# Two edits to an encoder layer: early residual rows stored through SP's queue, and the closing norm divided over VectorE, ScalarE and GpSimd

## The chip, the cores and the metric

The kernel runs on one core of one Trainium2 chip. A core has TensorE (PE, matmuls, with its weight loads shown apart as PEld), VectorE (DVE), ScalarE (ACT), GpSimd (POOL) and SyncE (SP). SP does no arithmetic here: it issues most of the DMAs, one after the other, in the order in which the program has them. GpSimd issues the indirect DMAs (gathers and scatters by a list of row numbers) and a few plain ones. The metric is device microseconds of one execution. The kernel before was timed three times: 889.92 us in the median (888.94 to 892.41).

## What is computed

One encoder layer on 1024 tokens of 1024 features, in float32:

```python
h  = x
hn = rms_norm(h, norm_mix_g);  proj = hn @ w_in            # q, k, v of both attentions
y_dil = dilated_mixture_attention(...)                      # 8 heads, 512 columns
y_na  = neighbourhood_attention(...)                        # 8 heads, 512 columns
h = h + concat(rms_norm(y_dil, g_out_dil), rms_norm(y_na, g_out_na)) @ w_out
h = h + hierarchical_moe(rms_norm(h, norm_ffn_g), ...)      # each token: 2 of 16 SwiGLU experts
return rms_norm(h, norm_final_g)                            # row * 1/sqrt(mean(row^2) + eps) * g
```

## The kernel before

A matmul is made of three: each operand is split into a high part (ScalarE, `L103`) and a low part (VectorE, or GpSimd for some weights, `L104`), and high x high, low x high and high x low are summed in PSUM. Tokens are handled in eight blocks of 128 rows; `acc_d` in DRAM holds the residual rows `h`.

**The output projection has two halves.** `early_out` (`L742` to `L762`) is the first: while the last attention heads run, it multiplies block T of `y_dil` with the upper half of `w_out`, 24 matmuls a block (`L750`), and VectorE adds the product to the x rows of the block (`L753`, two instructions of 512 columns). When a block is done, its rows go to `acc_d` by a plain DMA that GpSimd issues (`L760`), and then SP loads the x rows of block T + 2 (`x_load`, `L726`). The second half begins when the first has ended. Its function `load(T)` has SP read a block of `y_na` (two DMAs, `L1160`) and of `acc_d` (`L1163`); PE turns the `y_na` block by four transposes (`y_turn`, `L135`), ScalarE and VectorE split it, and 24 matmuls a block follow (`L1270`). Three blocks are loaded ahead, the next ones inside the loop.

**The order of the work is written out by hand.** The whole program is one straight order of statements, with no scheduler: an engine's instructions stand in its queue as the statements issue them, and each engine works off its queue in order. An instruction waits until the semaphores of what it depends on have come.

**The experts** run 16 in a row with PE as the busiest engine. Their rows are added to `acc_d` by indirect DMAs; the last two experts (14 and 15) add theirs in SBUF.

**The end of the kernel** is the final norm. Row blocks 0 to 7 are loaded from `acc_d`; blocks 8 to 11 are gathered rows of the tokens of experts 14 and 15 (two blocks each), to which the experts' last products are still added (`add_both`, `add_late`, `L1631`). For each block ScalarE sums the squares (`square`, `L1570`); an inverse root of their mean is formed, either on VectorE by a bit trick and three Newton steps (`inverse_root_steps`, for blocks 0 to 3) or as ScalarE's Sqrt and VectorE's reciprocal (the others); and `finish(t)` scales the rows by the root and by g in one VectorE instruction (`L1609`) and stores them. Blocks 0 to 5 are stored through SP (`L1613`). Blocks 6 and 7 go out by an indirect DMA of GpSimd that leaves out the tokens of experts 14 and 15 (the index `keep`), and blocks 8 to 11 by indirect DMAs as well (`put`, `L1461`), once the blocks stored through SP have landed.

Between them the statements of the last experts stand, so that their splits, adds and matmuls share the queues with the norm. A `bank` of PSUM with tag "o" exists twice: the two halves of one expert's product fill both, and the next product can't be begun before VectorE has added the earlier one (`L1631`).

Of the kernel before, what the change touches and what calls it, by code (L numbers as in the profile page):

```python
# [13 lines left out]
AF = mybir.ActivationFunctionType  # L14
ALU = mybir.AluOpType
# [57 lines left out]
def build(nc, tc, a, ctx, dbg=None):  # L73
# [21 lines left out]
    acc_d = dram("acc_d", [1024, 1024])  # L95
# [7 lines left out]
        nc.scalar.activation(hi, src, AF.Copy)  # L103
        (nc.gpsimd if pool else nc.vector).tensor_tensor(lo, src, f(hi), op=ALU.subtract)  # L104

    def inverse_root_steps(ss, r, t, scale):


        V = nc.vector
        V.tensor_scalar(ss, ss, scale, EPS, op0=ALU.mult, op1=ALU.add)  # L110
        yield
        V.tensor_scalar(r.bitcast(I32), ss.bitcast(I32), -0.5, float(0x5f3759df), op0=ALU.mult, op1=ALU.add)
        yield
        for _ in range(3):
            V.tensor_tensor(t, r, r, op=ALU.mult)
            yield
            V.scalar_tensor_tensor(t, t, -0.5, ss, op0=ALU.mult, op1=ALU.mult)
            yield
            V.scalar_tensor_tensor(r, t, 1.5, r, op0=ALU.add, op1=ALU.mult)
            yield  # L120

    def run(gen, n=1):
        for _ in range(n):
            next(gen, None)
# [20 lines left out]
    with ExitStack() as att:  # L145
# [27 lines left out]
        with ExitStack() as ph:  # L173
# [4 lines left out]
            def x_load(T):  # L178
                xs[T] = xp.tile([128, 1024], F32, name="xt", bufs=3)
                nc.sync.dma_start(xs[T], a["x"][0, T * 128:(T + 1) * 128, :])  # L180
# [519 lines left out]
        who, wlo, raws, yd, yt, hx = {}, {}, {}, {}, {}, {}  # L700
# [35 lines left out]
        def yd_rstd():  # L736

            yield from inverse_root_steps(rd, rr, rt_, 1.0 / 512)

        def early_out():  # L740

            for T in range(8):  # L742
                y = yt.pop(T)
                for c in range(2):
                    ps = bank("mm")
                    cc = slice(512 * c, 512 * c + 512)
                    i = 0
                    for k in range(4):
                        for l, w in ((0, who), (0, wlo), (1, who)):
                            nc.tensor.matmul(ps, y[:, l, k, :], w[0][:, k, cc], start=i == 0, stop=i == 11)  # L750
                            i += 1
                            if i == 12:
                                nc.vector.scalar_tensor_tensor(hx[T][:, cc], ps, rr[:, T:T + 1], hx[T][:, cc],  # L753
                                                               op0=ALU.mult, op1=ALU.add)
                            if T < 7 and 12 * c + i == 10:
                                yd_turn(T + 1)
                                if T < 5:
                                    yd_load(T + 3)
                            yield
                nc.gpsimd.dma_start(acc_d[128 * T:128 * T + 128, :], hx.pop(T))  # L760
                if T < 6:
                    x_load(T + 2)  # L762

        def g_out_load():
            for k, nm in ((0, "g_out_dil"), (4, "g_out_na")):
# [87 lines left out]
        for s in range(len(steps) + 4):  # L853
            at = s % 16
            before = pairs[s // 16 - 1] if s >= 16 else None
            if s < len(steps):
                p, h, n = steps[s]
# [83 lines left out]
    V = nc.vector  # L941
# [207 lines left out]
    with ExitStack() as ph:  # L1149
        op_ = ph.enter_context(tc.tile_pool(name="out", bufs=2))  # L1150
        y, h, yt, ht, rs, ry, pls = {}, {}, {}, {}, {}, {}, {}
# [212 lines left out]
    g_l = ex.tile([128, 1024], F32, name="g_l", bufs=1)  # L1364
# [60 lines left out]
    def act_in(act):  # L1425
        pt = bank("s")
        for k in range(2):
            nc.tensor.transpose(pt[:, k * 128:(k + 1) * 128], act[:, k * 128:(k + 1) * 128], ident)  # L1428
        ah = ex.tile([128, 256], F32R, name="a_hi")
        al = ex.tile([128, 256], F32R, name="a_lo")  # L1430
        split(ah, al, pt[:, 0:256])
        return ah, al
# [20 lines left out]
    def new_act():  # L1453
        return ex.tile([128, 256], F32, name="act", bufs=2)
# [30 lines left out]
    ss = ex.tile([128, 14], F32, name="ss_f", bufs=1)  # L1485
    hs, hr = {}, {}
# [82 lines left out]
    def square(t):  # L1569
        nc.scalar.activation(junk, hs[t // 2][:, t % 2], AF.Square, accum_out=ss[:, t:t + 1])  # L1570

    def inverse_root(*ts):
        c, n = ts[0], len(ts)
        r = ex.tile([128, 8], F32, name="r_f", bufs=2)[:, 0:n]
        tmp = ex.tile([128, 8], F32, name="t_f", bufs=1)[:, 0:n]
        for t in ts:
            hr[t] = r[:, t - c:t - c + 1]
        yield from inverse_root_steps(ss[:, c:c + n], r, tmp, 1.0 / 1024)

    def mean(*ts):  # L1580
        v = ss[:, ts[0]:ts[0] + len(ts)]
        V.tensor_scalar(v, v, 1.0 / 1024, EPS, op0=ALU.mult, op1=ALU.add)

    def inverse_root_last(*ts):
        c, n = ts[0], len(ts)
        v = ss[:, c:c + n]
        nc.scalar.activation(v, v, AF.Sqrt)
        r = ex.tile([128, 8], F32, name="r_l", bufs=3)
        V.reciprocal(r[:, 0:n], v)
        for t in ts:  # L1590
            hr[t] = r[:, t - c:t - c + 1]

    def late(t):

        return gi[:, t % 2, at(14 + (t - 8) // 2)]
# [3 lines left out]
    def put(idx, src, of_block):  # L1599
# [4 lines left out]
            tc.declare_no_dep(ins, before, reason="rows of other tokens")  # L1604
        indirect.append((ins, of_block))

    def finish(t, whole=False):
        h = hs[t // 2][:, t % 2]
        V.scalar_tensor_tensor(h, h, hr[t], g_l, op0=ALU.mult, op1=ALU.mult)  # L1609
        if t > 7:  # L1610
            put(late(t), h, False)
        elif whole or t < 6:
            stored.append(nc.sync.dma_start(a["out"][128 * t:128 * t + 128, :], h).ins)  # L1613
        else:
            put(keep[:, t:t + 1], h, True)
# [7 lines left out]
    def inverse_root_half():  # L1623
        nc.scalar.activation(ss[:, 13:14], ss[:, 13:14], AF.Sqrt, scale=1.0 / 1024, bias=ss[:, 12:13])
        r = ex.tile([128, 8], F32, name="r_l", bufs=3)
        V.reciprocal(r[:, 0:1], ss[:, 13:14])
        hr[11] = r[:, 0:1]
# [5 lines left out]
    def add_both(t, parts):  # L1633
        for z in range(2):
            add_late(t, z, parts[z])
# [40 lines left out]
    add_both(8, parts)  # L1676
    for t in range(4):
        square(t)
    acts[0] = new_act()
    expert_up(xs.pop(15), W[15], ws[:, 0, at(15)], acts[0])  # L1680
    run(inverse_root(0, 1, 2, 3), 100)
    square(8)
    square(4)
    finish(0)
    parts = [expert_down(aa, W[14], z) for z in range(2)]
    aa = act_in(acts[0])
    finish(1)
    add_both(9, parts)
    for t in (5, 6, 7, 9):
        square(t)  # L1690
    finish(2)
    acts[1] = new_act()
    expert_up(xs1, W[15], ws[:, 1, at(15)], acts[1])
    nc.scalar.activation(root, root, AF.Sqrt)
    mean(4, 5, 6, 7, 8, 9)
    inverse_root_last(4, 5, 6, 7, 8, 9)
    finish(3)
    parts = [expert_down(aa, W[15], z) for z in range(2)]
    aa = act_in(acts[1])
    add_both(10, parts)  # L1700
    square(10)
    finish(4)
    finish(5)
    parts = [expert_down(aa, W[15], z, tag="mm") for z in range(2)]
    mean(10)
    inverse_root_last(10)
    add_late(11, 0, parts[0])
    square_half(0)
    finish(8)
    add_late(11, 1, parts[1])  # L1710
    square_half(1)
    finish(6)
    finish(9)
    inverse_root_half()
    finish(11)
    finish(10)
    finish(7)

    ordered.close()

# [74 lines left out]
```

## Time and profile before

| | |
|---|---|
| three timed runs | 888.94, 889.92, 892.41 us |
| the profiled execution, its own time | 892.44 us |
| its span, from the first to the last instruction | 890.7 us |
| PE busy | 832.3 us (93% of the span) |
| PE weight loads | 693.2 us (78%) |
| DVE, ACT, POOL busy | 558.5 (63%), 510.0 (57%), 220.9 us (25%) |
| matmuls | 4492 |
| bytes moved by DMA | 168.72 MB |

The profiled execution is 2.5 us longer than the median of the timed ones. A matmul's end is modelled, so PE counts as busy while it streams; what one costs is read from the distance of the starts. The column PEclk gives the clock that TensorE was granted, as a share of 2.4 GHz: 1.00 is 2.4 GHz, 0.50 is 1.2 GHz. Line numbers are those of the kernel before; in the changed kernel the same statements stand up to 30 lines lower.

### The profile page before, as it was taken

Reading aid. Unit: us, or ns where it says so; the run is one execution under the profiler, and the core shown is the slowest. Engines: PE = TensorE matmul, PEld = TensorE weight load, DVE = VectorE, ACT = ScalarE, POOL = GpSimd, SP = SyncE. Lnnn points to the kernel's source line nnn. Section 1 sums busy time; section 2 is a strip of 40 time slices with the busy share of each in tenths; the row PEclk is TensorE's granted clock in tenths of the full one; section 3 lists DMA queues with packets and bytes.
Section 4 is the critical chain, followed back from the end, with each engine's and each line's share of the span. In section 5 each row is a group of like instructions: output and inputs, shape, how many; then the busy total and the mean of one; then the engine's idle time right before and its main releaser. Section 6 shows DMA issues by size and latency. Waiting matters only on the chain. (4 is left out here: it accounts for less than half of the span.)

```text
span 890.7 us, 13312 instructions
## 1 busy us (share of the span) xinstructions
PE 832.3 (93%) x4492; PEld 693.2 (78%) x4492; DVE 558.5 (63%) x1249; ACT 510.0 (57%) x1079; POOL 220.9 (25%) x180
## 2 busy tenths in 40 slices
PE   8999999989999999999898999999799999999880
PEld 5888878979889888878787887887577787777760
DVE  4551125776767767666677753677786566959573
ACT  5441127757667576677575633543585566858570
POOL 4001122221232302332411100000442344635403
PEclk8999999999999999999999999998999999999995
DMA  6855452314343141534346747995798987999663
GB/s 238 286 210 165 126 159 65 105 48 108 96 136 105 54 137 48 148 100 120 76 160 195 265 144 239 357 343 216 233 354 250 317 220 209 357 324 304 181 257 121
DMA packets 129919, 168.72 MB, mean 189 GB/s; under 512 B 14875, under 2 KB 101403, under 8 KB 129824
## 3 DMA queue, kind: packets, MB, share of 16 engines
q1 hardware_dynamic: 119904, 143.58, 49.8%
q0 software_dynamic: 9936, 24.16, 9.8%
q8 instruction: 41, 0.67, 0.3%
q14 instruction: 38, 0.31, 0.1%
HBM read 129.93 MB, written 47.47 MB: 199 GB/s over the span
## 5 line engine op out<-in xcount | busy, mean ns | idle before, releaser
L103 ACT ACTIVATE pt_hi<-ps_pt 128x512 fp32r<-128x512 f32 (+2 forms) x128 | 67.6, 528 | 70.8 <-PE ps_pt L509 41.7
L378 PE MATMUL ps_mm<-xhi,w_lo 128*128 128x512 f32 x256 | 105.1, 411 | 1.1 <-POOL w_lo L104 1.1
L378 PE MATMUL ps_mm<-xlo,w_hi 128*128 128x512 f32 x256 | 105.0, 410 | 0.0
L378 PE MATMUL ps_mm<-xhi,w_hi 128*128 128x512 f32 x256 | 102.9, 402 | 0.0
L104 DVE TENSOR_TENSOR pt_lo<-ps_pt,pt_hi 128x512 fp32r<-128x512 f32 (+2 forms) x128 | 77.2, 603 | 31.8 <-ACT pt_hi L103 31.1
L104 POOL TENSOR_TENSOR w_lo<-w_raw,w_hi 128x1024 fp32r<-128x1024 f32 x16 | 38.3, 2392 | 229.5 <-ACT w_hi L103 229.5
L424 DVE CUSTOM_DVE_ANT_0 p<-ps_s,bias 128x256 f32<-128x256 f32 (+1 forms) x192 | 81.8, 450 | 18.2 <-PE ps_s L411 10.8
L104 DVE TENSOR_TENSOR g_lo<-raw_up,g_hi 128x1024 fp32r<-128x1024 f32 x64 | 75.5, 1220 | 25.2 <-ACT g_hi L103 25.1
L1419 PE MATMUL ps_mm<-g_hi,x_hi 128*128 128x512 f32 x184 | 76.0, 413 | 0.5 <-ACT x_hi L103 0.5
L1419 PE MATMUL ps_mm<-g_hi,x_lo 128*128 128x512 f32 x184 | 74.2, 403 | 2.2 <-DVE x_lo L104 2.2
L1419 PE MATMUL ps_mm<-g_lo,x_hi 128*128 128x512 f32 x184 | 73.9, 402 | 0.0
L430 ACT ACTIVATE p<-p,stats 128x256 f32<-128x256 f32 x128 | 63.7, 500 | 9.6 <-DVE stats L424 9.1
L103 ACT ACTIVATE g_hi<-raw_up 128x1024 fp32r<-128x1024 f32 x64 | 64.4, 1067 | 1.8 <-DMA raw_up<-in_w_up 0.8
L411 PE MATMUL ps_s<-k_hh,q_s 128*128 128x256 f32 (+1 forms) x192 | 60.7, 324 | 4.0 <-DMA k_hh<-k_hh 1.4
L411 PE MATMUL ps_s<-k_low,q_s 128*128 128x256 f32 (+1 forms) x192 | 62.6, 334 | 0.0
L411 PEld LDWEIGHTS ps_s<-k_hh,q_s 128*128 128x128 f32 x192 | 44.6, 232 | 10.9 <-DVE q_s L402 2.6
L378 PEld LDWEIGHTS ps_mm<-xhi,w_lo 128*128 128x128 f32 x256 | 48.7, 190 | 5.2 <-POOL w_lo L104 1.4
L1357 POOL DMA_INDIRECT xg<-hn_d,gi x30 | 41.3, 1377 | 40.1 <-PEq L1533 9.3
L378 PEld LDWEIGHTS ps_mm<-xhi,w_hi 128*128 128x128 f32 x256 | 48.7, 190 | 3.2
L378 PEld LDWEIGHTS ps_mm<-xlo,w_hi 128*128 128x128 f32 x256 | 48.4, 189 | 3.5
L411 PEld LDWEIGHTS ps_s<-k_low,q_s 128*128 128x128 f32 x192 | 44.6, 232 | 3.5
L430 ACT ACTIVATE p<-p,nm 128x384 f32<-128x384 f32 (+1 forms) x64 | 37.5, 586 | 15.2 <-DVE nm L424 14.8
(301 smaller groups left out, 2125.6 us busy)
## 6 DMA issues: line engine op xcount, KB each, us to landing
raw_up<-in_w_gate SPq DMA_DIRECT2D x32, 512.0 KB
raw_up<-in_w_up SPq DMA_DIRECT2D x32, 512.0 KB
raw_down<-in_w_down SPq DMA_DIRECT2D x16, 1024.0 KB
w_raw<-in_w_in SPq DMA_DIRECT2D x16, 512.0 KB
xt<-in_x SPq DMA_DIRECT2D x8, 512.0 KB
k_hh<-in_w_in SPq DMA_DIRECT2D x8, 512.0 KB
va_d<-vt SPq DMA_DIRECT2D x16, 256.0 KB
vb_d<-vt SPq DMA_DIRECT2D x8, 512.0 KB
```

The lines of the kernel that those rows point to most:

```text
L103: nc.scalar.activation(hi, src, AF.Copy)
L104: (nc.gpsimd if pool else nc.vector).tensor_tensor(lo, src, f(hi), op=ALU.subtract)
L378: nc.tensor.matmul(ps, l[:, k, :], x[half][:, k, :], start=i == 0, stop=i == 23)
L411: nc.tensor.matmul(ps, self.q[h][:, qs], keys(k[h]), start=n == 0, stop=n == 1)
L424: nc.vector.tensor_tensor_reduce(out=p, in0=ps, in1=bias, scale=-0.125, scalar=3.0e38, op0=ALU.add, op1=ALU.min, accum_out=nm)
L430: nc.scalar.activation(p, p, AF.Exp, bias=nm, scale=-1.0, accum_out=l)
L1357: return nc.gpsimd.indirect_dma_start(out=x, out_offset=None, in_=src[:, :], in_offset=bass.IndirectOffsetOnAxis(ap=idx, axis=0), bounds_c ...
L1419: nc.tensor.matmul(ps, l[:, k, :], wt[:, k, :], start=i == 0, stop=i == 23)
```

## The change

1. **Rows stored through SP.** `early_out` no longer issues the store of block T from GpSimd at the end of the block. A new function `h_store(T)` issues it, and the x load after it, from SP, at the seventh matmul of block T + 1; block 7's store is issued when the loop has ended.
2. **Newton steps on GpSimd.** For blocks 0 to 3 the three Newton steps (nine VectorE instructions) become twelve GpSimd instructions of 128x4; the first two instructions of the root stay on VectorE.
3. **g ahead of the root.** For blocks 0, 1, 4, 5 and 8 VectorE multiplies the rows by g as soon as the squares are summed (`times_g`), and `finish` is then one ScalarE instruction that scales by the root. The other blocks finish as before.
4. **Order and destinations.** Blocks 2 to 7 are stored through SP, and blocks 0 and 1 go out with the index `keep`. The order of the statements changes: finish 2, 3, 4, 6, 5, 7, 0, 9, 8, 11, 1, 10 in place of 0, 1, 2, 3, 4, 5, 8, 6, 9, 11, 10, 7.

```diff
-    def inverse_root_steps(ss, r, t, scale):
+    def inverse_root_steps(ss, r, t, scale, pool=False):
...
         for _ in range(3):
+            if pool:
+                for o, a, b in ((t, r, r), (t, t, ss), (t, None, None), (r, r, t)):
+                    if a is None:
+                        nc.gpsimd.tensor_scalar(t, t, -0.5, 1.5, op0=ALU.mult, op1=ALU.add)
+                    else:
+                        nc.gpsimd.tensor_tensor(o, a, b, op=ALU.mult)
+                    yield
+                continue
             V.tensor_tensor(t, r, r, op=ALU.mult)
...
+        def h_store(T):
+            nc.sync.dma_start(acc_d[128 * T:128 * T + 128, :], hx.pop(T))
+            if T < 6:
+                x_load(T + 2)
...
+                            if T and 12 * c + i == 6:
+                                h_store(T - 1)
...
-                nc.gpsimd.dma_start(acc_d[128 * T:128 * T + 128, :], hx.pop(T))
-                if T < 6:
-                    x_load(T + 2)
+            h_store(7)
...
+    def times_g(t):
+        h = hs[t // 2][:, t % 2]
+        V.tensor_tensor(h, h, g_l, op=ALU.mult)
+        by_g.add(t)
...
-        V.scalar_tensor_tensor(h, h, hr[t], g_l, op0=ALU.mult, op1=ALU.mult)
+        if t in by_g and not whole:
+            nc.scalar.activation(h, h, AF.Copy, scale=hr[t])
+        else:
+            V.scalar_tensor_tensor(h, h, hr[t], g_l, op0=ALU.mult, op1=ALU.mult)
...
-        elif whole or t < 6:
+        elif whole or t > 1:
...
-    run(inverse_root(0, 1, 2, 3), 100)
+    run(inverse_root(0, 1, 2, 3, pool=True), 100)
     square(8)
     square(4)
-    finish(0)
+    times_g(8)
     parts = [expert_down(aa, W[14], z) for z in range(2)]
     aa = act_in(acts[0])
-    finish(1)
+    times_g(4)
+    finish(2)
+    square(5)
     add_both(9, parts)
-    for t in (5, 6, 7, 9):
+    for t in (6, 7, 9):
         square(t)
-    finish(2)
+    finish(3)
...
```

SP's queue where the first half of the output projection ends, in the kernel before. `k_hh<-in_x` is an x load, `y_na<-y` a store of attention rows, and `y<-y_na` and `h<-acc_d` are the loads of the second half:

```order
L695 DMA y_na<-y 128x4x128 [waits DVE_49]
L695 DMA y_na<-y 128x4x128 [waits DMAHW0_49,DVE_49]
L726 DMA k_hh<-in_x 128x1024 [waits PE_49]
L1160 DMA y<-y_na 64x1x512 [waits DMAHW2_49,DMAHW3_49,DMAHW0_49,DMAHW5_49,PE_49,DMAHW7_49,Activation_49,Pool_49]
L1160 DMA y<-y_na 64x1x512
L1163 DMA h<-acc_d 128x1024 [waits DMAHW4_49]
```

The same place in the changed kernel, with the stores of blocks 5, 6 and 7 (`acc_d<-k_hh`):

```order
L703 DMA y_na<-y 128x4x128 [waits DVE_49] x2
L749 DMA acc_d<-k_hh 128x1024 [waits DMAHW6_49,DMAHW0_49]
L734 DMA k_hh<-in_x 128x1024 [waits PE_49]
L749 DMA acc_d<-k_hh 128x1024 [waits DMAHW3_49,DVE_49]
L749 DMA acc_d<-k_hh 128x1024 [waits DMAHW7_49,DMAHW1_49,DVE_49]
L1173 DMA y<-y_na 64x1x512 [waits DMAHW2_49,DMAHW4_49,PE_49,DMAHW5_49,Activation_49,Pool_49]
L1173 DMA y<-y_na 64x1x512
L1176 DMA h<-acc_d 128x1024
```

The stores of blocks 6 and 7 now stand ahead of the first `y_na` load, and each waits for VectorE.

GpSimd's queue at the end, in the changed kernel, from the last gather of rows on. In the kernel before the first `spacer` memset of `put` follows the gather directly:

```order
L1370 DMA raw_up<-acc_d,gi 128x1024
L120 TENSOR_TENSOR t_f<-r_f 128x4 [waits DVE_49]
L120 TENSOR_TENSOR t_f<-t_f,ss_f 128x4 [waits Activation_49,Pool_49]
L118 ISA
L118 TENSOR_SCALAR t_f<-t_f 128x4 [waits Pool_49]
L120 TENSOR_TENSOR r_f<-r_f,t_f 128x4 [waits Pool_49]
L120 TENSOR_TENSOR t_f<-r_f 128x4 [waits Pool_49]
L120 TENSOR_TENSOR t_f<-t_f,ss_f 128x4 [waits Pool_49]
L118 TENSOR_SCALAR t_f<-t_f 128x4 [waits Pool_49]
```

Besides the arithmetic there is one instruction more, `L118 ISA`, which the diff does not show. It is put in ahead of the first `tensor_scalar` of GpSimd and reloads the engine's library of instructions. The kernel before has one such instruction, `L104 ISA`, ahead of its first GpSimd `tensor_tensor` at the start.

VectorE's queue at the end, in the kernel before, right behind the last Newton step (`raw_down` and `raw_up` are row blocks, `g_l` is g, `a_lo` a split of the last experts):

```order
L1609 SCALAR_TENSOR_TENSOR raw_down<-raw_down,r_f,g_l 128x1024 [waits DMAHW7_49,DVE_49]
L104 TENSOR_TENSOR a_lo<-ps_s,a_hi 128x256 [waits Activation_49]
L1609 SCALAR_TENSOR_TENSOR raw_down<-raw_down,r_f,g_l 128x1024 [waits DMAHW0_49]
L1631 TENSOR_TENSOR raw_up<-ps_o,raw_up 128x512 [waits DMASW5_49]
L1631 TENSOR_TENSOR raw_up<-ps_o,raw_up 128x512
```

And in the changed kernel, from the last instruction of the root that stays on VectorE:

```order
L112 TENSOR_SCALAR r_f<-ss_f 128x4 [waits DVE_49]
L1622 TENSOR_TENSOR raw_up<-raw_up,g_l 128x1024 [waits Activation_49]
L104 TENSOR_TENSOR a_lo<-ps_s,a_hi 128x256 [waits Activation_49]
L1622 TENSOR_TENSOR raw_up<-raw_up,g_l 128x1024 [waits DMAHW3_49]
L1633 SCALAR_TENSOR_TENSOR raw_up<-raw_up,r_f,g_l 128x1024 [waits DMAHW1_49,Pool_49]
L1655 TENSOR_TENSOR raw_up<-ps_o,raw_up 128x512 [waits DMASW5_49]
L1655 TENSOR_TENSOR raw_up<-ps_o,raw_up 128x512
```

The finish of block 2 (`L1633`) waits for GpSimd, and the two adds that free the PSUM banks stand right behind it.

## Rows read from the trace of the kernel before

**Rows 1.** Busy time by stretch (engine busy and instructions, PEclk, DMA share, GB/s).
```profile
570.00:600.00 30.00, 30.00 (x187) 25.84 (x187) 21.88 (x67) 14.03 (x31) 0.00 (x0) 1.00 0.99 349
700.00:800.00 100.00, 98.60 (x464) 78.13 (x463) 63.40 (x79) 61.80 (x96) 46.10 (x32) 1.00 0.91 283
```

**Rows 2.** SP's timeline where the second half begins (start, length, issue, count).
```profile
534.44 1.36 SPq L1160 DMA_DIRECT2D y<-y_na  x2
...
540.89 0.46 SPq L1163 DMA_DIRECT2D h<-acc_d  x1
...
550.84 0.33 SPq L1243 DMA_DIRECT2D small<-in_small  x1
```

**Rows 3.** All engines' timeline at the same place; brackets: idle before, and its releaser.
```profile
540.68 0.60 PE L135 MATMUL ps_pt<-ident,y 128*128 128x128 f32 x4
...
540.88 0.75 DVE L753 SCALAR_TENSOR_TENSOR k_hh<-ps_mm,rr,k_hh 128x512 f32<-128x512 f32 x1 [2.05 <-PE ps_mm L750]
...
541.93 0.53 POOL L760 DMA_DIRECT2D acc_d<-k_hh  x1 [5.07 <-DVE k_hh L753]
...
542.37 0.51 PE L1270 MATMUL ps_mm<-whi,yt_hi 128*128 128x512 f32 x1 [1.09 <-ACT yt_hi L103]
```

**Rows 4.** Busy time just behind the first load's issue.
```profile
535.00:536.00 1.00, 1.00 (x6) 0.79 (x5) 0.72 (x1) 0.00 (x0) 0.00 (x0) 1.00 0.14 23
536.00:537.00 1.00, 1.00 (x6) 0.80 (x5) 0.04 (x1) 0.00 (x0) 0.53 (x1) 1.00 0.42 135
```

**Rows 5.** Busy time where PE stood still and began again.
```profile
832.00:833.00 1.00, 0.00 (x0) 0.00 (x0) 1.00 (x2) 1.00 (x4) 1.00 (x1) 1.00 0.78 66
...
834.00:836.00 2.00, 1.77 (x6) 1.48 (x7) 1.71 (x4) 1.22 (x2) 1.51 (x4) 0.62 0.91 141
...
838.00:840.00 2.00, 2.00 (x10) 1.62 (x9) 2.00 (x3) 0.95 (x1) 0.36 (x2) 1.00 0.82 285
```

**Rows 6.** The chain that ended last, same place (start, length, what).
```profile
834.74 7.08 PE ps_mm L1419 x24
...
845.71 5.61 PE ps_mm L1419 x24
```

**Rows 7.** VectorE's timeline in the closing norm.
```profile
852.38 0.17 DVE L112 TENSOR_SCALAR r_f<-ss_f 128x4 int32<-128x4 int32 x1
...
854.36 1.28 DVE L1609 SCALAR_TENSOR_TENSOR raw_down<-raw_down,r_f,g_l 128x1024 f32<-128x1024 f32 x1
...
857.09 1.28 DVE L1631 TENSOR_TENSOR raw_up<-ps_o,raw_up 128x512 f32<-128x512 f32 x2
...
870.63 0.68 DVE L1631 TENSOR_TENSOR raw_up<-ps_mm,raw_up 128x512 f32<-128x512 f32 x1
```

**Rows 8.** The smallest copies on GpSimd, line 1526.
```profile
L1526 POOL COPY idx<-gi x14: 197/746/1712, 635.3 to 820.8; 128x1 int32<-128x1 int32 x14
```

**Rows 9.** GpSimd's timeline at the last stores.
```profile
871.52 1.88 POOL L1461 DMA_INDIRECT out<-raw_up,gi  x1 [28.06 <-DVE raw_up L1631]
...
873.70 0.98 POOL L1461 DMA_INDIRECT out<-raw_down,keep  x1 [0.19 <-DVE raw_up L1609]
...
874.99 0.96 POOL L1461 DMA_INDIRECT out<-raw_up,gi  x1 [0.19 <-issue]
...
878.80 0.96 POOL L1461 DMA_INDIRECT out<-raw_down,keep  x1 [0.19 <-issue]
```

**Rows 10.** GpSimd's instructions of line 104 (count, ns min/median/max, first and last start).
```profile
L104 POOLq EVENT_SEMAPHORE  x6: 17/30/1952, 12.6 to 129.0; - x6
...
L104 POOLq MODIFY_POOL_CONFIG  x2: 1/1/1, 5.2 to 5.2; - x2
```

**Rows 11.** PE's timeline at the last experts' products.
```profile
859.78 0.40 PE L1444 MATMUL ps_o<-d_hi,a_hi 128*128 128x512 f32 x1
...
862.58 0.38 PE L1428 MATMUL ps_s<-ident,act 128*128 128x128 f32 x2
```

**Rows 12.** ScalarE's copy with a scale by rows, line 716.
```profile
L716 ACT ACTIVATE whi<-w_raw,g_out x4: 1139/1147/1157, 454.9 to 495.5; 128x1024 fp32r<-128x1024 f32 x4
```

More of the change, by code (lines that the diff above doesn't have):

```diff
@@ L1570, in square, with inverse_root @@
         nc.scalar.activation(junk, hs[t // 2][:, t % 2], AF.Square, accum_out=ss[:, t:t + 1])
-    def inverse_root(*ts):
+    def inverse_root(*ts, pool=False):
         c, n = ts[0], len(ts)
@@ L1577, in inverse_root @@
             hr[t] = r[:, t - c:t - c + 1]
-        yield from inverse_root_steps(ss[:, c:c + n], r, tmp, 1.0 / 1024)
+        yield from inverse_root_steps(ss[:, c:c + n], r, tmp, 1.0 / 1024, pool)
     def mean(*ts):
@@ L1605, in put @@
         indirect.append((ins, of_block))
+    def times_g(t):
+        h = hs[t // 2][:, t % 2]
+        V.tensor_tensor(h, h, g_l, op=ALU.mult)
+        by_g.add(t)
+    by_g = set()
     def finish(t, whole=False):
         h = hs[t // 2][:, t % 2]
-        V.scalar_tensor_tensor(h, h, hr[t], g_l, op0=ALU.mult, op1=ALU.mult)
+        if t in by_g and not whole:
+            nc.scalar.activation(h, h, AF.Copy, scale=hr[t])
+        else:
+            V.scalar_tensor_tensor(h, h, hr[t], g_l, op0=ALU.mult, op1=ALU.mult)
         if t > 7:
             put(late(t), h, False)
-        elif whole or t < 6:
+        elif whole or t > 1:
             stored.append(nc.sync.dma_start(a["out"][128 * t:128 * t + 128, :], h).ins)
@@ L1678, in build @@
         square(t)
+    times_g(0)
+    times_g(1)
     acts[0] = new_act()
     expert_up(xs.pop(15), W[15], ws[:, 0, at(15)], acts[0])
-    run(inverse_root(0, 1, 2, 3), 100)
+    run(inverse_root(0, 1, 2, 3, pool=True), 100)
     square(8)
     square(4)
-    finish(0)
+    times_g(8)
     parts = [expert_down(aa, W[14], z) for z in range(2)]
     aa = act_in(acts[0])
-    finish(1)
+    times_g(4)
+    finish(2)
+    square(5)
     add_both(9, parts)
-    for t in (5, 6, 7, 9):
+    for t in (6, 7, 9):
         square(t)
-    finish(2)
+    finish(3)
     acts[1] = new_act()
@@ L1695, in build @@
     mean(4, 5, 6, 7, 8, 9)
+    times_g(5)
     inverse_root_last(4, 5, 6, 7, 8, 9)
-    finish(3)
+    finish(4)
     parts = [expert_down(aa, W[15], z) for z in range(2)]
     aa = act_in(acts[1])
+    finish(6)
     add_both(10, parts)
+    finish(5)
     square(10)
-    finish(4)
-    finish(5)
+    finish(7)
     parts = [expert_down(aa, W[15], z, tag="mm") for z in range(2)]
     mean(10)
+    finish(0)
     inverse_root_last(10)
@@ L1708, in build @@
     square_half(0)
-    finish(8)
     add_late(11, 1, parts[1])
     square_half(1)
-    finish(6)
     finish(9)
     inverse_root_half()
+    finish(8)
     finish(11)
+    finish(1)
     finish(10)
-    finish(7)
     ordered.close()
```

## The prediction

> **What bounds the kernel now.** I read the stretches first. From the second half of the output projection to the last expert PE never rests: 30.00 us busy of 30 in one stretch, 98.60 of 100 in the expert loop, with the clock at 1.00 [rows 1]. So whatever stops PE there by a microsecond makes the kernel a microsecond longer; nothing later gives it back. The timelines came next, for the two places that the change touches: the start of the second half [rows 2 to 4], and the closing norm [rows 7 to 12], where VectorE, ScalarE and GpSimd hand work to each other and the last matmuls wait for them. The first is in the middle of the kernel and is the one that is easily missed. All sums are made on the profiled execution (892.44 us, span 890.7) and then moved to the median of 889.92, which is 2.5 lower.
>
> **Part 1, the stores through SP.** What SP gains is eight issues of about 0.46 us each, read from a load of the same 512 KB [rows 2], against 0.53 that GpSimd spends on one now [rows 3]. Until block 6 this costs nothing: PE is full of attention work and x loads are needed a block later. The last two stores are different. SP works its queue in order, and the stores of blocks 6 and 7 now stand ahead of the six `y_na` loads with which the second half begins. Block 7's store waits for VectorE's last add, which starts at 540.88 and takes 0.75 [rows 3]: 541.63. In the kernel before, the first `y_na` load was issued at 534.44 [rows 2], 7.2 us sooner, so that PE could turn the block at 540.68, directly behind the first half's last matmul [rows 3].
>
> Now SP issues the store at 541.63 (0.46), then the two halves of the block (1.36 for both [rows 2]), the second from 542.8 on. How long a load needs is read from the one of before: issued at 534.44, with the engines moving 23 GB/s until 536 and 135 GB/s in the microsecond after [rows 4]. Data move some 1.6 us behind the issue and are there after perhaps 2.5. I take 2.5, so 545.3. The bounds are 1.6 (no data were seen sooner) and 4.0 (2.5 and the 512 KB of the store ahead of it at the 349 GB/s of rows 1, 1.5 us). From the turn to the first matmul it was 540.68 to 542.37, 1.7 us [rows 3]; so the first matmul starts at 547.0 instead of 542.37, 4.6 later (3.7 to 6.1).
>
> PE stands still for four microseconds of this. Where it did so before, it restarted at a lower clock: no matmul and still 1.00 at 832 to 833, then 0.62 at 834 to 836 and 1.00 again from 838 [rows 5], which is 1.2 and 2.4 GHz; 24 matmuls took 7.08 us there and 5.61 at full clock [rows 6], 1.5 more. Part of the slow time falls on the splits here, so I take 1.3 (0 to 1.5). **Term 1: 4.6 + 1.3 = 5.9 us (3.7 to 7.6).**
>
> A rule speaks against this term. The Trainium skill (DMA: Bandwidth & Descriptors, section Issuing engines are not separate DMA queues) says that all DMAs end on the same 16 engines, and that the choice of the issuing engine saves only sequencer time. By that rule alone part 1 would be free. The trace does not contradict it, but rows 2 show what it leaves out: SP's `small` load was issued 9 us behind the load ahead of it, because the queue stood still.
>
> **Part 2, Newton steps on GpSimd.** VectorE ends the part that it keeps at 852.38 + 0.17 = 852.55 and before was through with the Newton steps at 854.36, where the first finish began [rows 7]. GpSimd now does twelve small operations. The trace has no such arithmetic on GpSimd; the nearest row is a copy of one column, 0.197 at the least and 0.746 in the median, when others were under way [rows 8]. With the 0.19 that lies between GpSimd's instructions [rows 9] as an upper mark for the gap I take 0.3 each (0.2 to 0.9), so 3.6 in all.
>
> After the first two comes the instruction that the diff does not show, the reload of the library. At the start of the kernel its like stands at 5.2, and the next instruction of GpSimd's sequencer begins at 12.6 [rows 10]: 7.4 us, hidden there, because the first GpSimd subtraction waits for ScalarE anyway. I take 7.4; the low bound is 0, since that row does not prove that the sequencer had nothing else to wait for. The Trainium skill (GPSIMD Engine Reference, section Instruction dispatch) tells of about 6 us for the first call to a freshly loaded kernel, with nothing in the profile to be seen. With its 6 the term would be 1.4 smaller; the trace agrees in kind with its 7.4.
>
> So the root is there at 852.55 + 0.6 + 7.4 + 3.0 = 863.6. VectorE's finish of block 2 waits for it, in order, and behind it stand the two adds that were at 857.09 [rows 7]. They free the PSUM banks that PE's next product needs, at 859.78 [rows 11]. With 1.2 for the finish and 0.65 for the first add PE goes on at 865.4, 5.6 later. It has stood still for over five microseconds and pays the lower clock, 1.5 [rows 6]. The transposes of the last product come at 869.7 instead of 862.58 [rows 11], and all that follows hangs on them. **Term 2: 5.6 + 1.5 = 7.1 us (0 to 8.5).** Its zero is exact below a point: VectorE reaches that finish at about 856.4 anyhow, and PE loses nothing while the root is there by about 857.5.
>
> **Parts 3 and 4, the finishes.** Before, GpSimd's six stores follow each other from 871.52 to 878.80, about 1.3 apart [rows 9]; they and VectorE's five finishes after the last add (870.63 [rows 7]) end together. Now three of these finishes are VectorE's and two ScalarE's, at 1.15 each [rows 12], and the first store goes out early. Five stores behind the last add (871.3) and one finish (1.2) put the last at 872.6 + 4 x 1.28 = 877.7, a gain of 1.1. Against it, one ScalarE finish now stands ahead of a split that PE waits for, and a VectorE finish ahead of the adds of block 10, 1.2 each, partly in waits. I set the sum at 0 (-1.1 to 1.2). Multiplying by g ahead of time costs VectorE four or five passes while it waits for ScalarE, and for the root.
>
> **The sum.** 892.44 + 5.9 + 7.1 + 0 = 905.4 for the profiled execution; on the median **902.9 us**.
>
> **The rivals.**
> - *The reload is free* because the library is already there. For it: the two instructions themselves show 1 ns [rows 10]. Against it: the 7.4 us behind them, at a time when the library should have been there as well. Then only term 1 stays: 889.92 + 5.9 = 895.8.
> - *The store does not hold the `y_na` loads* up by anything that PE feels, as the rule of part 1 has it: only an issue each. Against it is the order of SP's queue. Then term 2 alone: 897.0.
> - *Not slower.* Both waits stay hidden: the load of block 0 lands before 541 and the root is there before 857.5; then the early first store decides, at GpSimd's pace of 1.3 [rows 9], and the kernel gains the 1.1 of parts 3 and 4: 888.8. It needs two things that the order and rows 10 speak against.
>
> **How the numbers follow.** My forecast, both waits, 0.62, with its own range 899 to 906 (3.7 + 5.5 to 7.6 + 8.5). Reload free 0.18, no hold-up 0.09, neither 0.05. What is left, 0.06, is mostly longer waits than my bounds. The range of 8 in 10 takes in the first two rivals: 895 to 907. A change under 0.5%, 4.4 us, cannot be told from none here. The forecast and both single-wait rivals lie above 894.4, with most of what is left: slower 0.93; neither wait gives no change, 0.05; faster 0.02.
>
> **What would show it.** Step by step: the first `y_na` load issued at or after the last add of the first half, and PE idle for about five microseconds before its first matmul, with a lower clock behind it; in the closing norm about seven microseconds between GpSimd's second small multiply and its first `tensor_scalar`, VectorE idle until then, and PE idle before the product that stood at 859.78. If PE goes straight from one half to the other, term 1 is wrong; if GpSimd's twelve steps follow at 0.3 each, term 2 is.

## The result and the profile after

The changed kernel takes 900.29 us in the median (899.39 to 901.64, four runs), the kernel before 889.43 on the same chip (888.55 to 892.41): 1.0117 times as long, 95% interval 1.009 to 1.0145, which is 10.4 us (8.0 to 12.9). Forecast were 13.0 more. The profiled execution took 899.39 us, with a span of 897.6.

**Start of the second half.** SP's timeline of the changed kernel shows the queue standing still (start, length, issue, count). The two stores that were put ahead of the loads form one row, which ends when the store of block 7 is issued; the first `y_na` load was issued at 534.44 before [rows 2]:

```profile
535.41 5.92 SPq L749 DMA_DIRECT2D acc_d<-k_hh  x2
541.56 1.35 SPq L1173 DMA_DIRECT2D y<-y_na  x2
```

All engines at the same place, to be read against [rows 3] (brackets: the idle time before, and what ended it):

```profile
539.80 0.40 PE L763 MATMUL ps_mm<-whi,w_hi 128*128 128x512 f32 x1
540.24 0.75 DVE L766 SCALAR_TENSOR_TENSOR k_hh<-ps_mm,rr,k_hh 128x512 f32<-128x512 f32 x1 [2.05 <-PE ps_mm L763]
...
546.95 1.08 PE L143 MATMUL ps_pt<-ident,y 128*128 128x128 f32 x4 [6.75 <-issue]
...
549.12 0.80 PE L1283 MATMUL ps_mm<-whi,yt_hi 128*128 128x512 f32 x1 [1.09 <-ACT yt_hi L103]
```

The first line is PE's last matmul of the first half; in the kernel before it stands at

```profile
540.45 0.40 PE L750 MATMUL ps_mm<-whi,w_hi 128*128 128x512 f32 x1
```

VectorE's last add ends at 540.99, and then it is 6.0 us until PE turns the first block and 8.1 until its first matmul. What moved, and TensorE's clock, stand in the stretches (engine busy and instructions, PEclk, DMA share, GB/s):

```profile
542.00:543.00 1.00, 0.00 (x0) 0.00 (x0) 0.00 (x0) 0.00 (x0) 0.00 (x0) 1.00 1.08 418
...
544.00:546.00 2.00, 0.00 (x0) 0.00 (x0) 0.00 (x0) 0.00 (x0) 0.00 (x0) 0.50 0.99 225
...
549.00:551.00 2.00, 1.88 (x4) 1.45 (x5) 0.76 (x2) 1.97 (x5) 0.00 (x0) 0.50 0.99 314
551.00:553.00 2.00, 2.00 (x6) 1.61 (x5) 0.17 (x1) 0.19 (x1) 0.00 (x0) 0.50 1.07 262
553.00:555.00 2.00, 2.00 (x9) 1.54 (x9) 0.75 (x1) 0.00 (x0) 0.00 (x0) 0.87 0.67 223
```

At 542 to 543 the DMA engines move 418 GB/s; the 512 KB of the store that was issued just ahead of the load had landed by 543.7, as its semaphore tells in the trace. PE stands from 540.2 to 546.95; the granted clock is still 1.00 (2.4 GHz) at 542 to 543, 0.50 (1.2 GHz) from 544 on and through PE's first matmuls, and 0.87 over the stretch from 553. Matmul by matmul PE lags the kernel before by 6.3 us at the turn, by 6.8 at the first matmul and by 8.5 four microseconds later. As it was 0.65 us ahead at the last matmul of the first half (539.80 against 540.45), this place costs it 9.1.

**The closing norm.** GpSimd's timeline, with the Newton steps:

```profile
858.52 0.20 POOL L120 TENSOR_TENSOR t_f<-r_f 128x4 f32<-128x4 f32 x1 [9.90 <-DVE r_f L112]
858.79 1.20 POOL L120 TENSOR_TENSOR t_f<-t_f,ss_f 128x4 f32<-128x4 f32 x1
860.08 0.19 POOL L118 TENSOR_SCALAR t_f<-t_f 128x4 f32<-128x4 f32 x1
860.35 0.20 POOL L120 TENSOR_TENSOR r_f<-r_f,t_f 128x4 f32<-128x4 f32 x1
860.63 1.14 POOL L120 TENSOR_TENSOR t_f<-r_f 128x4 f32<-128x4 f32 x1
861.85 0.20 POOL L120 TENSOR_TENSOR t_f<-t_f,ss_f 128x4 f32<-128x4 f32 x1
...
863.52 0.20 POOL L120 TENSOR_TENSOR r_f<-r_f,t_f 128x4 f32<-128x4 f32 x1
```

Between the second multiply and the first `tensor_scalar` lie 0.09 us and not seven: the reload shows nowhere. But two of the twelve took 1.2 and 1.1 us in place of 0.20. VectorE's timeline says when:

```profile
858.70 1.23 DVE L1622 TENSOR_TENSOR raw_up<-raw_up,g_l 128x1024 f32<-128x1024 f32 x1 [0.27 <-ACT xg L1583]
...
860.50 1.22 DVE L1622 TENSOR_TENSOR raw_up<-raw_up,g_l 128x1024 f32<-128x1024 f32 x1
863.76 1.28 DVE L1633 SCALAR_TENSOR_TENSOR raw_up<-raw_up,r_f,g_l 128x1024 f32<-128x1024 f32 x1 [2.04 <-POOL spacer L1614]
864.96 1.28 DVE L1655 TENSOR_TENSOR raw_up<-ps_o,raw_up 128x512 f32<-128x512 f32 x2
```

The two long ones end at 859.99 and 861.77, 0.05 and 0.06 us behind the ends of VectorE's multiplies by g (859.93 and 861.72). The finish of block 2 waits 2.04 us for GpSimd, and the adds that free PE's banks follow it. PE's waits in this part (engine, line, tile, releaser; us in total, times, longest):

```profile
PE ps_mm L1457 <- ACT a_hi L103: 2.0, 1, 2.0
PE ps_o L1457 <- DVE raw_up L1655: 0.5, 1, 0.5
```

The second is the wait of term 2, 0.5 us. The first, 2.0, stands at a place that had 0.5 before, where it was PE's only wait in this part:

```profile
PE ps_mm L1444 <- ACT a_hi L103: 0.5, 1, 0.5
```

The 2.0 is read on ScalarE's timeline:

```profile
866.32 1.06 ACT L1583 ACTIVATE xg<-raw_up 128x1024 f32<-128x1024 f32 x1 [2.80 <-issue]
...
867.38 0.36 ACT L1435 ACTIVATE sg<-ps_mm 128x256 f32<-128x256 f32 x1
...
869.61 1.15 ACT L1631 ACTIVATE raw_up<-raw_up,r_l 128x1024 f32<-128x1024 f32 x1 [0.26 <-DVE r_l L1602]
870.67 0.36 ACT L103 ACTIVATE a_hi<-ps_s 128x256 fp32r<-128x256 f32 x1
```

The square of block 9 had to wait for the late adds; the sigmoid of the last expert stood behind it (867.38, though PE had begun the last matmul of the product at 864.87), and then ScalarE's finish of block 4 (869.61) stood ahead of the split (870.67). The first of the last twelve matmuls, before and now:

```profile
863.44 0.50 PE L1444 MATMUL ps_mm<-d_hi,a_hi 128*128 128x512 f32 x1 [0.47 <-ACT a_hi L103]
```

```profile
871.08 0.79 PE L1457 MATMUL ps_mm<-d_hi,a_hi 128*128 128x512 f32 x1 [2.04 <-ACT a_hi L103]
```

So the lag of PE, 5.3 us ahead of these products, grew by 0.7 for the banks and by 1.6 for the split, to 7.6. The last twelve matmuls then ran partly at the lower clock, which put the last one 9.1 behind. The last stores are

```profile
876.38 1.05 POOL L1474 DMA_INDIRECT out<-raw_down,keep  x1 [12.63 <-SPq L1760]
...
881.14 0.98 POOL L1474 DMA_INDIRECT out<-raw_up,gi  x1 [3.59 <-SPq L1760]
...
886.24 0.97 POOL L1474 DMA_INDIRECT out<-raw_up,gi  x1 [0.19 <-issue]
```

The last store does not show the 1.5 us of the lower clock: it started 15.4 us behind the first of the last twelve matmuls before (863.44 to 878.80 [rows 9]), and 15.2 now (871.08 to 886.24). Counted from the last matmul it is 12.7 before and 11.0 now, but only because that matmul came late. Five stores follow each other at 1.27; the first of them waited until 880.2 for the landing of the last store through SP, which SP had issued at 875.10.

### The profile page after: what moved, and what is told of

Its sections match the earlier page's. It is cut to its first block, busy times and chain, and to the rows that moved or that the text cites. A ratio compares the mean times of both kernels' runs of the same rounds, so it can differ in the third digit from the quotient of the medians.

```text
span 897.6 us, 13286 instructions
## 1 busy us (share of the span) xinstructions
PE 831.2 (93%) x4492; PEld 693.0 (77%) x4492; DVE 557.7 (62%) x1240; ACT 515.1 (57%) x1084; POOL 215.4 (24%) x184
## 5 line engine op out<-in xcount | busy, mean ns | idle before, releaser
L104 DVE TENSOR_TENSOR pt_lo<-ps_pt,pt_hi 128x512 fp32r<-128x512 f32 (+2 forms) x128 | 77.2, 603 | 31.8 <-ACT pt_hi L103 31.0
L104 POOL TENSOR_TENSOR w_lo<-w_raw,w_hi 128x1024 fp32r<-128x1024 f32 x16 | 38.3, 2394 | 229.3 <-ACT w_hi L103 229.3
L104 DVE TENSOR_TENSOR g_lo<-raw_up,g_hi 128x1024 fp32r<-128x1024 f32 x64 | 75.5, 1220 | 25.6 <-ACT g_hi L103 25.6
L1370 POOL DMA_INDIRECT xg<-hn_d,gi x30 | 37.9, 1264 | 36.5 <-PEq L1546 9.3
L438 ACT ACTIVATE p<-p,nm 128x384 f32<-128x384 f32 (+1 forms) x64 | 37.5, 586 | 14.6 <-DVE nm L432 14.2
```

The costliest lines, as they stand in the source:

```text
L438: nc.scalar.activation(p, p, AF.Exp, bias=nm, scale=-1.0, accum_out=l)
L1370: return nc.gpsimd.indirect_dma_start(out=x, out_offset=None, in_=src[:, :], in_offset=bass.IndirectOffsetOnAxis(ap=idx, axis=0), bounds_c ...
```

## The experiments

Theory at the start: the SP queue costs 8.5 us and stays (S), the closing norm adds about 2 and not 7. Rival (G): the lag of PE against the first profile fell from 8.5 to 5.3 us by the last experts, so 3 us are given back further on, and the closing norm must hold 5. All kernels but two were timed beside the kernel before; it had medians of 890.51 to 890.64 us there. The expected times start from 889.4, so they are to be read as differences.

**Closing norm alone.** `early_out` is the one of the kernel before.

```diff
...
-                            if T and 12 * c + i == 6:
-                                h_store(T - 1)
...
-            h_store(7)
+                nc.gpsimd.dma_start(acc_d[128 * T:128 * T + 128, :], hx.pop(T))
+                if T < 6:
+                    x_load(T + 2)
```

> Only the closing norm is changed; the stores are GpSimd's again. Theory S (the wait of SP's queue costs 8.5 us at the start of the second half and nothing gives it back; the 3 us by which the lag shrinks later are the lateness of the one profiled execution of the kernel before): the tail is worth +1.6 to +2.4, so 891.0 to 891.8. Theory G (idle time further on gives back 3 us of the 8.5 in any execution, so the stores are worth 5.4): the tail must hold the other 5.4, so about 894.9.

Measured: 893.28 us, ratio 1.0032 (1.0021 to 1.0043), +2.8 us. Near S, which had 1.6 to 2.4, and well below the 5.4 of G. In its profile PE waits 1.6 us for the banks and 2.1 for the split; its last twelve matmuls then run at 1.00 (2.4 GHz), and the last store starts 15.1 us behind the first of them, as in the changed kernel. So the lower clock of the changed kernel's last matmuls belongs to that execution and moved nothing behind it.

**Stores through SP alone**, in the kernel before.

```diff
+        def h_store(T):
+            nc.sync.dma_start(acc_d[128 * T:128 * T + 128, :], hx.pop(T))
...
-                nc.gpsimd.dma_start(acc_d[128 * T:128 * T + 128, :], hx.pop(T))
...
+            h_store(7)
```

> The kernel before with the stores through SP alone. Theory S: 889.4 + 8.5 = 897.9. Theory G: 889.4 + 5.4 = 894.8. In both PE's turn of block 0 starts about 5.5 us behind the last add of the first half, as in the changed kernel.

Measured: 897.83 us, ratio 1.0092 (1.0075 to 1.0109), +8.2 us by the ratio (6.7 to 9.7), +7.3 by the medians. The two parts add up to the whole within their intervals: 2.8 and 8.2 against 10.4. The 5.4 of G is out; the 8.5 of S lies in the interval.

**The kernel before, profiled once more**, to see where the 3 us of G came from.

> The kernel before, profiled once more, to see where one execution of it differs from another. Theory S (what the lag of the changed kernel seemed to give back was lateness of the first profiled execution): at least one of the three stretches 610 to 620, 630 to 640 and 830 to 840 us, where that execution had a granted clock of 0.66, 0.83 and 0.83, stands at another clock here, and the time lies at 888.5 to 891. Theory G (the places give time back in any execution): the same three stretches at the same clock, and 892 again.

Measured, in one execution: 890.94 us. The three stretches in the first profile, and then in this one:

```profile
610.00:620.00 10.00, 9.05 (x54) 7.23 (x54) 8.54 (x45) 3.64 (x6) 1.85 (x2) 0.66 0.62 236
630.00:640.00 10.00, 7.78 (x28) 5.88 (x29) 7.79 (x11) 5.56 (x7) 5.01 (x4) 0.83 0.72 230
830.00:840.00 10.00, 7.69 (x32) 6.10 (x31) 8.14 (x10) 7.75 (x11) 7.41 (x9) 0.83 0.65 132
```

```profile
610.00:620.00 10.00, 7.03 (x85) 6.31 (x84) 8.72 (x48) 3.64 (x6) 1.81 (x2) 1.00 0.53 210
630.00:640.00 10.00, 7.83 (x30) 6.13 (x30) 7.51 (x9) 5.31 (x7) 4.23 (x4) 0.83 0.81 267
830.00:840.00 10.00, 8.11 (x33) 6.43 (x32) 8.73 (x10) 6.15 (x9) 6.43 (x10) 0.83 0.79 162
```

The first is at 1.00 now; here the clock was low at 620 to 626 instead (0.72, and 1.00 in the first profile). Between 610 and 640, where PE waits for the routing again and again, the two executions have their low stretches at different places. Against this execution, PE of the kernel with the stores alone lags by 9.5 us at the start of the second half and by 7.5 ahead of the last products, and PE of the changed kernel by 8.7 and 6.9, where the first profile gave 5.3.

One execution is thus a poor measure of what is given back, but the traces of all fourteen can be set side by side: ten in which no store of blocks 6 and 7 goes through SP, four in which both do (in one of them block 7 in two halves). From PE's last matmul of the first half to its turn of the second `y_na` block it is 6.25 to 6.26 us in each of the ten, and 15.4 to 15.8 in the four: the place costs 9.1 to 9.6. From that turn to the last matmul ahead of the last experts' products it is 308.4 to 312.9 us in the ten, 310.6 in the mean, and 309.5 to 311.4 in the four, 310.4 in the mean. So no time is seen to be given back, as the prediction had it, and G's three microseconds were the lateness of one execution; a microsecond given back would be hidden in this spread. The 8.2 (6.7 to 9.7) of the timed runs goes with either.

**Newton steps back on VectorE**, everything else changed.

```diff
-    run(inverse_root(0, 1, 2, 3, pool=True), 100)
+    run(inverse_root(0, 1, 2, 3), 100)
```

> The changed kernel with the Newton steps on VectorE. My reading of the trace (no reload to be seen, GpSimd's twelve steps took 5.2 us, VectorE's finish of block 2 would start only 0.6 us sooner, as two multiplies by g then stand behind the steps): 0.6 to 1.0 under the changed kernel, 899.3 to 899.7. Rival, the forecast's term 2 (GpSimd's steps cost 7.1): 893 to 894.

Measured: 900.74 us, ratio 1.0113 (1.0097 to 1.013), against 1.0117 of the changed kernel: the 7.1 of term 2 are out, and the 0.6 to 1.0 expected do not show, which these intervals could also hide. VectorE's timeline shows why it is little:

```profile
862.40 1.22 DVE L1622 TENSOR_TENSOR raw_up<-raw_up,g_l 128x1024 f32<-128x1024 f32 x1
...
863.87 1.22 DVE L1622 TENSOR_TENSOR raw_up<-raw_up,g_l 128x1024 f32<-128x1024 f32 x1
865.00 1.28 DVE L1633 SCALAR_TENSOR_TENSOR raw_up<-raw_up,r_f,g_l 128x1024 f32<-128x1024 f32 x1
```

Its root is there at 862.48, but the two multiplies by g (`L1622`) stand ahead of the finish all the same. From the last instruction of the root that both kernels have on VectorE (`L112`, begun at 860.54 here and at 858.26 in the changed kernel) to the finish it is 4.5 us, and 5.5 in the changed kernel: at this place GpSimd's steps cost 1.0.

**Blocks 6 and 7 alone stored by GpSimd**, in the changed kernel.

```diff
-            nc.sync.dma_start(acc_d[128 * T:128 * T + 128, :], hx.pop(T))
+            (nc.sync if T < 6 else nc.gpsimd).dma_start(acc_d[128 * T:128 * T + 128, :], hx.pop(T))
```

> The changed kernel, with the stores of blocks 6 and 7 alone issued by GpSimd, the other six still by SP. If only the two stores ahead of the first y_na loads cost: the same as the kernel with the closing norm alone changed (891.0 to 891.8 by theory S). If stores through SP cost all along (x loads or stores of attention rows behind them): 895 or more.

Measured: 894.0 us, ratio 1.0031 (1.0016 to 1.0046), the same as with no store through SP (1.0032), though above the 891.8 expected, as that one was. Within these intervals the first six stores cost nothing, and the last two all.

**Half the bytes ahead of the load.** The first 512 columns of block 7 are stored when they are ready.

```diff
+                            if T == 7 and 12 * c + i == 14:
+                                nc.sync.dma_start(acc_d[896:1024, 0:512], hx[7][:, 0:512])
...
-            h_store(7)
+            nc.sync.dma_start(acc_d[896:1024, 512:1024], hx.pop(7)[:, 512:1024])
```

> The changed kernel, with the first 512 columns of block 7 stored when they are ready, so that only 256 KB instead of 512 KB stand directly ahead of the first y_na load. Theory 'bytes' (the load is late behind the bytes of the store, which moved at 418 GB/s): from the end of the load's issue to the first turn 3.3 to 3.4 us in place of 4.0. Rival 'latency' (a load needs 4 us whatever stands ahead): 4.0 again. The whole time moves by less than one look can tell, 899 to 901.

Measured, in one execution: 903.56 us, which decides nothing about the time. SP's timeline, then PE's:

```profile
543.33 1.35 SPq L1175 DMA_DIRECT2D y<-y_na  x2
```

```profile
548.20 1.08 PE L143 MATMUL ps_pt<-ident,y 128*128 128x128 f32 x4 [6.18 <-DMA y<-y_na]
```

From 544.68, the end of the issue, to the turn it is 3.5 us; in the changed kernel 542.91 to 546.95, 4.0. But the kernel with the stores alone has 4.0 and the one with the Newton steps back 3.8, with the same 512 KB ahead. So half the bytes took off 0.3 to 0.5 of the 0.6 to 0.7 expected, in one execution, where the same bytes differ by 0.2; neither theory is shown. The semaphores in the traces say more: the second half of the block landed 3.8 us behind its issue here, 4.1 to 4.4 in the three executions with 512 KB ahead, and 3.6 to 4.8 in the nine executions of kernels that store all blocks through GpSimd. There no store stands directly ahead, though an x load, issued 3.7 us sooner in the first profile, landed only behind the issue of this one. So about 4 us are what this load takes in these kernels; in the kernel before they were hidden behind PE's work.

**No multiplies by g for blocks 8 and 4**, in the kernel with the closing norm alone changed.

```diff
-    times_g(8)
...
-    times_g(4)
```

> As the kernel with the closing norm alone changed (893.3), without the multiplies of blocks 8 and 4 by g; those two finish on VectorE in one instruction. Theory 'multiplies' (VectorE's two multiplies stretch GpSimd's steps from 3.3 to 5.2 us and stand ahead of the adds that PE waits for): the twelve steps take 3.3 to 3.5 us, PE loses nothing before the product of the last but one expert, the split of ScalarE follows at once; 890.0 to 891.3. Rival 'GpSimd' (its steps are long by themselves): 5 us again, 892.7 to 893.3.

Measured: 890.86 us, ratio 1.0006 (0.9995 to 1.0017), and in a second series 890.99, ratio 1.0000 (0.9983 to 1.0016). The 2.8 us are gone, as far as these intervals tell. The edit does more than it shows: without its multiply a block is finished by VectorE, so ScalarE's finish of block 4 no longer stands ahead of the split either. GpSimd's first and last step:

```profile
848.73 0.20 POOL L120 TENSOR_TENSOR t_f<-r_f 128x4 f32<-128x4 f32 x1 [8.72 <-DVE r_f L112]
...
851.84 0.20 POOL L120 TENSOR_TENSOR r_f<-r_f,t_f 128x4 f32<-128x4 f32 x1
```

Twelve steps in 3.3 us, none long, and PE's waits are

```profile
PE ps_mm L1452 <- DVE a_lo L104: 0.8, 1, 0.8
PE ps_mm L1452 <- ACT a_hi L103: 0.5, 1, 0.5
```

Nothing waits for the banks any more, and ScalarE's split is 0.5 late as in the kernel before; VectorE's, behind the finish of block 4, is now 0.8 late. The second series had this expectation:

> The kernel without the multiplies of blocks 8 and 4 once more, beside the two others of this call: 890 to 891.5, as its first runs (890.86).

It came out so.

**ScalarE's finish of block 4 behind the split**, in the kernel with the closing norm alone changed.

```diff
-    finish(4)
     parts = [expert_down(aa, W[15], z) for z in range(2)]
     aa = act_in(acts[1])
+    finish(4)
```

> As the kernel with the closing norm alone changed (893.3), with ScalarE's finish of block 4 behind the split of the last expert's activations instead of ahead of it. Theory 'split late': PE's wait for that split falls from about 2.0 to 1.0 us and the time by 0.7 to 1.1, 892.2 to 892.6. Rival 'end set elsewhere' (the last stores wait for the landing of the stores through SP, not for PE): 893.3.

Measured: 892.07 us, ratio 1.0016 (1.0004 to 1.0028), 1.2 to 1.4 less, with intervals that overlap. PE's wait for the split is 0.7 in its profile, 2.1 in that of the closing norm alone, so the finish did stand in the way.

**Newton steps on GpSimd alone**, in the kernel before.

```diff
-    run(inverse_root(0, 1, 2, 3), 100)
+    run(inverse_root(0, 1, 2, 3, pool=True), 100)
```

> The kernel before with the Newton steps on GpSimd alone. GpSimd's twelve steps take 3.3 us at 0.28 each, as VectorE does nothing meanwhile, in place of VectorE's 1.8; the finish of block 0 waits, the split behind it too. Theory 'small': PE's product waits about 1 us, 891 to 892. Rival 'reload' (the forecast's term 2): 895 or more, with seven microseconds ahead of the first tensor_scalar. Rival 'hidden': 890.5.

Measured: 893.16 us, ratio 1.0028 (1.0015 to 1.0041), +2.5 us; more than "small" had it, far from "reload". The twelve steps took 3.3 us here too. VectorE's finish of block 0, and PE's waits:

```profile
854.25 1.28 DVE L1617 SCALAR_TENSOR_TENSOR raw_down<-raw_down,r_f,g_l 128x1024 f32<-128x1024 f32 x1 [3.40 <-POOL spacer L1609]
```

```profile
PE ps_o L1452 <- DVE raw_up L1639: 1.1, 1, 1.1
PE ps_mm L1452 <- DVE a_lo L104: 0.7, 1, 0.7
PE ps_mm L1452 <- ACT a_hi L103: 0.6, 1, 0.6
```

2.4 us of waits, in place of 0.5: the finish waits 3.4 us for GpSimd, and the adds and the split stand behind it. In the kernel without the two multiplies the same steps cost nothing that shows. By the order of its queue the split stands ahead of the finish there, and one finish, not two, ahead of the adds; that this is the reason was not tested by itself.

**Stores of blocks 0 and 1 early.** As the kernel without the two multiplies; ScalarE finishes both while it waits for the sum of block 9.

```diff
...
+    finish(0)
+    finish(1)
+    square(9)
...
```

> As the one without the multiplies of blocks 8 and 4, with ScalarE finishing blocks 0 and 1 while it waits for the sum of block 9, so that GpSimd's stores of these two go out some 10 us sooner and four stores instead of five follow the late adds. Theory 'stores at the end' (GpSimd's pace of 1.3 us a store and the landing of SP's stores set the end): 1.3 to 2.5 under the one without the multiplies, 888 to 889.5. Rival 'ScalarE late' (its two finishes hold the square of block 9 and the sigmoid behind it): 891 or more.

Measured: 891.66 us, ratio 1.0014 (0.9997 to 1.0032): no gain, and the 888 to 889.5 of "stores at the end" are missed. GpSimd's first late store:

```profile
871.25 0.96 POOL L1469 DMA_INDIRECT out<-raw_up,gi  x1 [12.96 <-SPq L1754]
```

It waits for the landing of SP's last store, issued at 864.77; and the square of block 9 began 7.3 us behind the first Newton step, 5.9 without the two finishes ahead of it. So the steps of both theories are seen in the trace, and the time went as the rival had it.

**Destinations turned round**, also without the two multiplies. Blocks 0 to 4 go through SP early, 5 to 7 by GpSimd; block 0 is finished ahead of the square of block 9, block 1 behind the last split, block 4 behind VectorE's split.

```diff
-        elif whole or t > 1:
+        elif whole or t < 5:
...
```

> As the one without the multiplies of blocks 8 and 4, with the destinations turned round: blocks 0 to 4 through SP, finished early (block 0 by ScalarE before the square of block 9, block 1 behind the last split), blocks 5, 6 and 7 by GpSimd's indirect stores, and the finish of block 4 behind the split of VectorE. Theory 'stores at the end' (the late stores wait for the landing of the last store of SP, which comes 5 us behind its issue): the first late store leaves as soon as block 9 is finished, the last one 1.5 to 2.5 us sooner behind PE's last matmul than the 12.3 of that kernel, 888 to 889.5. Rival 'VectorE' (its queue of finishes and adds sets the end whatever the stores do): 890 to 891.

Measured: 890.03 us, ratio 0.9996 (0.9979 to 1.0014). The late stores no longer wait for SP:

```profile
870.70 1.65 POOL L1469 DMA_INDIRECT out<-raw_up,gi  x1 [2.17 <-DVE r_l L1645]
...
875.20 0.97 POOL L1469 DMA_INDIRECT out<-raw_up,gi  x1 [0.19 <-issue]
```

The last one starts 11.4 us behind the last matmul's start (863.78), 0.9 sooner than without this (12.3), less than expected; but in that kernel the third of the last twelve matmuls waited 0.8 for VectorE's split, and here it did not: counted from the first of the twelve it is 14.1 (861.11) against 16.0, 1.9 sooner. The time does not show it beyond its interval. VectorE's finish of block 9 began only at 868.91, behind the late adds, which is the rival's case, as is the time (890 to 891). No version beat the kernel before beyond its interval.

## Why the prediction came out as it did

The range and the sign held, and the time was 2.6 us too long. But two terms were off in opposite ways, so the nearness of the sum is luck: term 1 was right in kind, and the larger term 2 stood on a step that did not happen.

**Term 1, 5.9 us: right in kind, too small.** SP's queue held the load nearly as worked out (0.57 us between the last add and the load's issue, against 0.46), and the rest was too small. The largest miss is the load: from the issue of the block's second half to the turn I took 2.5, with 4.0 as the bound that had the store's 512 KB ahead; it was 4.7 (542.28 to 546.95), and 4.2 in the execution with half of these bytes. I had read the first moved bytes [rows 4] and guessed the landing. The trace before holds it: the second half of the same block, issued at 535.17, landed at 539.35 by its semaphore, 4.2 us later, with PE busy all the while. The step "from the turn to the first matmul, 1.7" was read at full clock [rows 3] and took 2.2 at the lower one (the four transposes 1.08 against 0.60). The lower clock itself then cost 1.7 instead of 1.3. With the 0.65 by which PE was ahead this place costs 9.1, and of the 3.2 more than forecast the load is 2.2. Measured alone, over the whole kernel, part 1 is 8.2 us (6.7 to 9.7), where 7.6 was the top of my bounds. "Until block 6 this costs nothing" held. The rule weighed there, of the Trainium skill (DMA: Bandwidth & Descriptors, section Issuing engines are not separate DMA queues), held for six stores and not for the last two, which cost 8 us by what stands behind them in the queue.

**Term 2, 7.1 us: the step of the reload was wrong.** From 7.4 us in GpSimd's sequencer at the start [rows 10] I took a price of the instruction. In the closing norm it cost less than 0.09, so the row at the start showed something else, which no run here tells. (The Trainium skill, GPSIMD Engine Reference, section Instruction dispatch, has its 6 us for a kernel freshly loaded; here, long behind the first `tensor_tensor` of GpSimd (14.6 us), this trace shows none of them.) The rival "the reload is free" was right in this, and wrong in the zero that it left for the closing norm. Its other step, twelve instructions at 0.3, was right for ten; two were held up by VectorE. PE lost 0.5 at the place named, not 5.6; in the other traces of this closing norm with GpSimd's steps that wait is 1.6, 1.1, 0.7 and next to none, and with the steps back on VectorE none.

**Parts 3 and 4, set at 0: wrong.** Multiplying by g was said to fill time in which VectorE waits. The multiplies of blocks 8 and 4 stand in that time by the clock, but ahead of the finish and the adds in the queue, and they stretch GpSimd's steps. Without them, and so without ScalarE's finish of block 4 ahead of the split, the 2.8 us of the closing norm are gone. That finish was named as a cost of up to 1.2, and paid: moved behind the split, 1.2 to 1.4 us come back, with intervals that overlap, and PE's wait falls from 2.1 to 0.7. How the rest divides between the longer steps and the places in VectorE's queue is not shown. Of the gain of 1.1 by the early first store 0.2 came, counted from the first of the last twelve matmuls to the last store; the late stores waited for the landing of SP's last one instead. With the destinations turned round, where they do not, it is 14.1 us against the 15.4 of the kernel before.

So the true course was the rival "reload free", which had a chance of 0.18, with its 5.9 at 8.2 and its zero at 2.8.

## What to carry to other kernels

Before a DMA is moved to another engine's queue, list what stands behind it there and what it waits for: a store whose data come late holds every load behind it, and the time that the load itself takes is then no longer hidden. Read that time to its landing, and not to the first moved bytes. Work that is put into an engine's idle time is free only if nothing that others wait for stands behind it in that queue, nor on another engine whose instructions lengthen while it runs. Undo one part at a time before you believe a sum that came out nearly right.

## What was not expected of the hardware

- The instruction `L118 ISA` that reloads GpSimd's library cost at most 0.09 us in the closing norm, long behind the first `tensor_tensor` of GpSimd (14.6 us).
- GpSimd's `tensor_tensor` of 128x4 took 0.20 us, but 1.20 and 1.14 when it began while VectorE multiplied 128x1024 by g, and ended 0.05 to 0.06 us behind that. The traces of four more runs with these multiplies have two such steps each (1.09 to 1.20, one of them a `tensor_scalar`). In the kernels where VectorE did no such multiply then, all twelve took 0.19 to 0.20. The Trainium skill (SBUF — State Buffer, section SBUF: two separate sides) says that VectorE and GpSimd share a pair of ports, and that a VectorE instruction with two inputs in SBUF keeps GpSimd out for its whole length; the trace agrees to 0.06 us. The forecast had not weighed it.
- A store of 512 KB issued by SP at 875.10 had landed at 880.2 only, with others in flight; the one of block 7, issued at 541.02, had landed at 543.7.
- Two executions of the kernel before had low clock at different places between 610 and 640 us, and PE of the one was 3.6 us ahead of the other's at 620, 1.5 at 630 and 1.6 at the end; so a lag of PE is read at several places, and against more than one profile.
